# Rotary angles made on quarter rows during the gate products, and a reordered opening and attention fill, in a one-core hybrid-encoder kernel

## The chip, the core and the metric

The kernel runs on one core of a Trainium2 chip. The time is the device time of one execution, in microseconds (us); a figure for a kernel is the median of several executions. Engines are named as the profile names them: PE (TensorE, matrix products), PEld (its weight loads), DVE (VectorE), ACT (ScalarE), POOL (GpSimd) and SP (SyncE, which here only issues transfers). ACT and POOL issue transfers too. Each engine works through its instructions in order.

## The reference

One encoder layer over 512 tokens of width 2048, all in float32. h is the RMS-normalised input; one projection of h gives every branch its input. Branch A is a bidirectional state-space scan; branch B is attention with low-rank queries and keys and a rotary part; the two are gated, summed, projected and added to the input, with a last RMS norm.

```
h = rmsnorm(x, norm_w);  u = h @ w_in
z_ssm, xbc, dt_f, dt_b, q_a, kv_a, z_attn, g_ssm, g_attn = split(u)
y  = ssd(fwd) + flip(ssd(bwd)) + d_skip * xs
y  = grouped_rmsnorm(y * silu(z_ssm))
q  = rmsnorm(q_a) @ w_uq          # 16 heads x (128 plain + 64 rotary)
kv = rmsnorm(c_kv) @ w_ukv        # 16 heads x (128 key + 128 value)
qr, kr = apply_rope(qr, cos, sin), apply_rope(kr, cos, sin)   # ang = position * inv
o  = softmax((qn kn' + qr kr') / sqrt(192)) v * silu(z_attn)
out = rmsnorm(x + (sig(g_ssm)*(y @ w_ps) + sig(g_attn)*(o @ w_pa)) @ w_out)
```

## The kernel before, in words

Every float32 operand of a product is split into a rounded high part and the remainder (tile names ending in `_h` and `_l`, or `wh` and `wl`), and a product is three products of the parts. For a weight chunk (`wchunk`, L157 to L165; `w_split` later) SP loads `wraw` (512 KB, three buffers), ACT casts it to `wh` (L163 or L433), and DVE, or POOL in the very first chunks, subtracts to `wl` (L164 or L434). All activations are held transposed, 128 features by 512 tokens.

PE executes in the order in which the program is written. The other engines' instructions are put in order by a scheduler, by priority: program order, with some helpers moved ahead (`tc.high_priority`). `keep_in_program_order` pins one of them.

The stages, in the order of the program:

- **Opening** (L195 to L242). Four token tiles `xt` are loaded by SP in halves of 512 KB; ACT sums squares (L210) and takes the root (L185); DVE makes the reciprocal root with a Newton step (L187 to L191) and scales (L220), ACT scales the second half of the last two tiles (L218). PE transposes sixteen feature tiles into eight PSUM banks (`x_turn`, L225), and `x_out` evicts each on ACT (`h_h`, L229) and DVE (`h_l`, L230). Constants `cst` and `vec` are loaded ahead of x on ACT's queue. Then follows the product that gives the time steps, `dtp` (48 matmuls through L168 to L170).
- **xbc products and sums.** Six products `xbc`, their convolution, the sums of h that the next stage needs (`h_sums`), and `dt_make`, a chain of some 20 operations on 64 rows by 512 for the softplus of the time steps.
- **Gates.** Three 2048x2048 products by a Strassen scheme (`Strassen.pair`, products named P1, P5, P6, P2, P3, P7, P4, all through L579 to L581). In P5 each chunk of weights X is first changed in place by an accumulating transfer of POOL's queue, split by DVE, and then added to Y by DVE (L696), and in P6 to another chunk (L700).
- **State-space groups** 0 to 3, filled up on PE with xbc, qkv and za products (`fill`).
- **Rotary angles and attention's start** (L1140 to L1220). The positions are broadcast to 128 partitions, and DVE makes the angles, wraps them twice and ACT takes their sine and cosine (`sinT`, `cosT`, L1197 and L1199), with 120 units of fill between; k is rotated (`kra`, `krb`).
- **Attention**, 16 heads. For each of four token tiles `scores` (five matmuls into `s`, L1326 to L1330; maximum on DVE, exponential on ACT, sum and scaling `pr` on DVE, L1332 to L1337), then `trans` (four transposes of `pr` into `pb`, L1348, evicted by ACT and DVE), and `pv` with the head before. Between them `some(unit)` lets the fill queue issue so many matmuls: the coming heads' q and k products (`qk_gen`), the rotary q part (`rope_gen`) and the values (`v_gen`, 256 columns per matmul, L1265 to L1267). A head starts with `fill.until(("qk", hd))`. In the last two heads the queue is empty; then the first product of the next Strassen scheme is the fill. At head 14 the program loads and splits x11 and x12 of y (`xraw` tiles, cast on ACT into the tiles that the trace names x__12841 and x__13011).
- **Projections and output** by Strassen schemes again.

Of the kernel before, what the change touches and what calls it, by code (L numbers as in the profile page):

```python
# [18 lines left out]
P = 128  # L19
# [53 lines left out]
def build(tc, a):  # L73
# [46 lines left out]
    dt_d, kr_d = scratch("dt_d"), dr.tile([64, SEQ], F32, name="kr_d")  # L120

# [11 lines left out]
    act.dma_start(cst, a["cst"])  # L133
    act.dma_start(vec, a["vec"])
# [22 lines left out]
    def wchunk(src, n):  # L157
        with tc.high_priority(offset=ahead[0]):
            raw = wp.tile([P, 1024], F32, tag="wraw", bufs=3, name="wraw")[:, :n]
            nc.sync.dma_start(raw, src)  # L160
            h = wp.tile([P, 1024], F32R, tag="wh", bufs=3, name="wh")[:, :n]
            l = wp.tile([P, 1024], F32R, tag="wl", bufs=3, name="wl")[:, :n]
            act.copy(h, raw)  # L163
            (dve if ahead[0] else pool).tensor_sub(l, raw, h.bitcast(F32))  # L164
        return h, l  # L165
# [37 lines left out]
    for t in range(TT):  # L203
        xt = xp.tile([P, D], F32, name=f"xt{t}")
        ss = few(2)
        for i in range(2):
            cs = slice(i * D // 2, (i + 1) * D // 2)
            nc.sync.dma_start(xt[:, cs], a["x"][t * P:(t + 1) * P, cs])
            scr = xp.tile([P, D // 2], F32, tag="scr", bufs=1, name="scr")
            act.activation(scr, xt[:, cs], AF.Square, accum_out=ss[:, i:i + 1])  # L210
        v = few(1)
        dve.tensor_add(v, ss[:, 0:1], ss[:, 1:2])
        dve.tensor_scalar(v, v, 1.0 / D, EPS, ALU.mult, ALU.add)
        r = small_rsqrt(v, 1, lambda n: few(1))
        for i in range(2):
            cs = slice(i * D // 2, (i + 1) * D // 2)
            if t >= TT - 2 and i == 1:
                act.activation(xt[:, cs], xt[:, cs], AF.Copy, scale=r)  # L218
            else:
                dve.tensor_scalar_mul(xt[:, cs], xt[:, cs], r)  # L220
        xs_t.append(xt)
    tps = [mm(), mm(), mm(), pa(), pa(), pb(), pb(), pc()]

    def x_turn(k, t):
        pe.transpose(tps[k % 8][:, t * P:(t + 1) * P], xs_t[t][:, k * P:(k + 1) * P], ident)  # L225

    def x_out(k):
        nw = vec[:, V_NORM + k:V_NORM + k + 1]
        act.activation(h_h[:, k, :], tps[k % 8], AF.Copy, scale=nw)  # L229
        dve.scalar_tensor_tensor(h_l[:, k, :], tps[k % 8], nw, h_h[:, k, :].bitcast(F32), ALU.mult, ALU.subtract)  # L230

    for t in range(TT - 1):
        for k in range(8):
            x_turn(k, t)
    for k in range(8):
        x_turn(k, TT - 1)
        x_out(k)
    for k in range(8):
        tps[k] = (mm, mm, mm, pa, pa, pb, pb, pc)[k]()
        for t in range(TT):  # L240
            x_turn(8 + k, t)
        x_out(8 + k)  # L242
# [4 lines left out]

    def in_gemm(tile_i, n="mm"):
        return gemm(mm(n), win(tile_i), h_h, h_l)

# [19 lines left out]
    dtp = in_gemm(T_DT, "dtp")  # L270
    ahead[0] = AHEAD
    da_d = dr.tile([64, SEQ], F32, name="da_d")
    dv_, dt64 = sxd("dv_"), sxd("dt64")
    act.activation(dv_[0:64, :], dtp[0:64, :], AF.Identity, bias=vec[0:64, V_DTB:V_DTB + 1])
    act.copy(dv_[64:128, :], dtp[64:128, :])
    put(kr_d, dv_[64:128, :])

    def dt_make(new):

        v = dv_[0:64, :]  # L280
        e, u, pl, da64 = (new(n)[0:64, :] for n in ("e", "u", "pl", "da64"))
# [13 lines left out]
        dve.scalar_tensor_tensor(dt64[0:64, :], pl, 2.0, v, ALU.mult, ALU.add)  # L295
        dve.tensor_scalar_mul(an, an, -1.0)
        dve.tensor_scalar_mul(da64, dt64[0:64, :], an)
        act.copy(dt64[64:128, :], da64)
        act.dma_start(da_d[0:NH, :], da64[0:NH, :])
        chunked = lambda t: t[NH:64, :].rearrange("p (c l) -> p c l", c=TT)  # L300
        dve.tensor_mul(chunked(pl), chunked(dt64)[:, :, ::-1], an[NH:64, :].unsqueeze(2).broadcast_to([NH, TT, P]))
        act.dma_start(da_d[NH:64, :], pl[NH:64, :])
        put(dt_d, dt64)
# [97 lines left out]
    def za_gen(i):  # L401
# [3 lines left out]
        act.activation(g_, p_, AF.Silu)  # L405
# [422 lines left out]

    gates[2].hooks = {(1, "P3"): [dt_back], (1, "P7"): [h_back, lambda: [h_part("x21", 256, q) for q in range(2)]]}
# [42 lines left out]
    dve.tensor_scalar_mul(vneg, vec[:, V_SN + 8:V_SN + 16], -1.0)  # L872
# [940 lines left out]
```

## Time and profile before

| what | value |
|---|---|
| three runs | 2007.54, 2008.22, 2011.87 us; median 2008.22 |
| the profiled execution's own time | 2010.63 us |
| its span (first to last instruction) | 2008.8 us |
| mean granted PE clock | 0.992 |
| busy: PE, DVE, ACT, POOL | 1941.0, 1481.6, 1032.3, 250.1 us |
| moved by DMA | 382.78 MB, mean 191 GB/s |

The profiled execution spent 1.8 us outside its span, and it was 2.4 us slower than the median of the three runs. In rows of the timeline the first number is the start and the second the duration, both in us; what stands in brackets is how long the engine sat idle before, and whom it waited for. Matmuls are pipelined, so the time of one is the distance to the next start and not its duration.

### The profile page before, as it was taken

The page shows a single profiled execution, that of the slowest core. Times are in us where ns is not written, and L with a number is a line of the kernel's source. Part 1 is how long each engine was busy: PE and PEld are TensorE (multiplying, and loading weights), DVE is VectorE, ACT ScalarE, POOL GpSimd, SP SyncE. Part 2 cuts the span into 40 slices and gives each one's busy share as a digit, 9 for nine tenths or more (in the row PEclk, how much of TensorE's full clock was granted, in tenths as well). Part 3 has the DMA queues.
Part 4 walks back from the last instruction along what each step waited for, and adds up shares of the span by engine and source line. Part 5 has one row for each costly group of instructions (what it writes and reads, how often), then busy time and mean ns, then how long its engine had stood idle before and what let it go on. Part 6 is the DMA issues. An engine that isn't in the chain of part 4 may idle for free.

```text
span 2008.8 us, 24843 instructions
## 1 busy us (share of the span) xinstructions
PE 1941.0 (97%) x9026; PEld 1606.9 (80%) x9026; DVE 1481.6 (74%) x2064; ACT 1032.3 (51%) x1527; POOL 250.1 (12%) x315
## 2 busy tenths in 40 slices
PE   6999999999999999999999999999979999999997
PEld 4888888888878878887878788888867787888886
DVE  7976676676659879798794767666666898879466
ACT  6444445444464757757666344444444455444243
POOL 0001001001012020120200101112112111100011
PEclk9999999999999999999999999999989999999998
DMA  5468558558444635665454956877998687857446
GB/s 189 163 192 215 152 131 220 139 134 226 130 153 142 194 122 164 213 187 181 151 173 137 271 153 177 223 202 220 236 254 297 213 290 283 277 169 242 163 88 158
DMA packets 168907, 382.78 MB, mean 191 GB/s; under 512 B 16272, under 2 KB 65552, under 8 KB 168592
## 3 DMA queue, kind: packets, MB, share of 16 engines
q1 hardware_dynamic: 103248, 233.61, 35.3%
q0 software_dynamic: 30656, 103.30, 23.3%
q10 hardware_dynamic: 34880, 44.28, 6.2%
q8 instruction: 71, 1.16, 0.2%
q14 instruction: 52, 0.43, 0.1%
HBM read 329.22 MB, written 98.04 MB: 213 GB/s over the span
## 4 chain that ended last, share of the span: by engine, by line
PE 75%; DVE 10%; DMA 8%; issue 3%; ACT 3%; POOL 0%; SPq 0%; ACTq 0%; DVEq 0%; POOLq 0%
PE P L580 11%; PE P L581 11%; PE P L579 11%; PE xbc L168 3%; PE xbc L169 3%; PE xbc L170 3%; DMA wraw<-wps 2%; PE za L170 2%; PE za L168 2%; PE za L169 2%; PE qkv L168 1%; PE qkv L170 1%; PE qkv L169 1%; PE f L1582 1%; PE f L1581 1%
## 5 line engine op out<-in xcount | busy, mean ns | idle before, releaser
L433 ACT CAST wh<-X 128x1024 fp32r<-128x1024 f32 x164 | 172.9, 1056 | 198.4 <-PE P L581 152.2
L434 DVE TENSOR_TENSOR wl<-X,wh 128x1024 fp32r<-128x1024 f32 x164 | 200.1, 1224 | 91.2 <-ACT wh L433 90.8
L164 DVE TENSOR_TENSOR wl<-wraw,wh 128x1024 fp32r<-128x1024 f32 (+2 forms) x148 | 172.6, 1167 | 91.6 <-ACT wh L163 86.1
L163 ACT CAST wh<-wraw 128x1024 fp32r<-128x1024 f32 (+2 forms) x150 | 145.1, 970 | 120.3 <-PE xbc L169 37.7
L434 DVE TENSOR_TENSOR wl<-Y,wh 128x1024 fp32r<-128x1024 f32 x88 | 107.6, 1224 | 69.7 <-ACT wh L433 69.6
L168 PE MATMUL xbc<-h_h,wh 128*128 128x512 f32 x384 | 153.3, 399 | 0.0
L433 ACT CAST wh<-Y 128x1024 fp32r<-128x1024 f32 x88 | 92.8, 1056 | 115.9 <-PE P L581 105.8
L170 PE MATMUL xbc<-h_h,wl 128*128 128x512 f32 x384 | 150.3, 391 | 0.0
L169 PE MATMUL xbc<-h_l,wh 128*128 128x512 f32 x384 | 150.1, 391 | 0.0
L579 PE MATMUL P<-wh,h_h 128*128 128x512 f32 x384 | 149.4, 389 | 0.0
L580 PE MATMUL P<-wl,h_h 128*128 128x512 f32 x384 | 149.4, 389 | 0.0
L581 PE MATMUL P<-wh,h_l 128*128 128x512 f32 x384 | 149.4, 389 | 0.0
L433 ACT CAST wh<-wraw 128x1024 fp32r<-128x1024 f32 x68 | 71.8, 1055 | 120.4 <-PE P L581 63.5
L434 DVE TENSOR_TENSOR wl<-wraw,wh 128x1024 fp32r<-128x1024 f32 x68 | 83.2, 1224 | 66.5 <-ACT wh L433 66.5
L580 PE MATMUL P<-wl,S 128*128 128x512 f32 x288 | 112.3, 390 | 0.5 <-DVE wl L434 0.5
L579 PE MATMUL P<-wh,S 128*128 128x512 f32 x288 | 112.1, 389 | 0.0
L581 PE MATMUL P<-wh,S 128*128 128x512 f32 x288 | 112.1, 389 | 0.0
L170 PE MATMUL za<-h_h,wl 128*128 128x512 f32 x256 | 100.1, 391 | 2.0 <-DVE wl L164 2.0
L168 PE MATMUL za<-h_h,wh 128*128 128x512 f32 x256 | 101.6, 397 | 0.0
L169 PE MATMUL za<-h_l,wh 128*128 128x512 f32 x256 | 99.7, 389 | 0.0
L1335 ACT ACTIVATE pr<-s,nm 128x512 f32<-128x512 f32 x64 | 44.2, 690 | 82.9 <-DVE nm L1333 82.2
L170 PEld LDWEIGHTS xbc<-h_h,wl 128*128 128x128 f32 x384 | 72.3, 188 | 15.6
(748 smaller groups left out, 5188.6 us busy)
## 6 DMA issues: line engine op xcount, KB each, us to landing
wraw<-wi SPq DMA_DIRECT2D x102, 512.0 KB, 3.7
da<-da_d SPq DMA_DIRECT2D x64, 256.0 KB, 4.1
T_wps<-wps POOLq DMA_DIRECT2D x32, 512.0 KB, 9.5
T_wpa<-wpa POOLq DMA_DIRECT2D x32, 512.0 KB, 11.4
wraw<-wps SPq DMA_DIRECT2D x24, 512.0 KB, 6.7
wraw<-wo SPq DMA_DIRECT2D x20, 512.0 KB, 3.5
xbc_d<-xbc ACTq DMA_DIRECT2D x24, 256.0 KB, 2.3
wraw<-wun SPq DMA_DIRECT2D x16, 384.0 KB, 6.1
```

What stands on the lines that cost most here:

```text
L163: act.copy(h, raw)
L164: (dve if ahead[0] else pool).tensor_sub(l, raw, h.bitcast(F32))
L168: pe.matmul(out, wh, xh, start=start, stop=False)
L169: pe.matmul(out, wh, xl, start=False, stop=False)
L170: pe.matmul(out, wl, xh, start=False, stop=stop)
L433: i = act.copy(hi_, raw)
L434: dve.tensor_sub(lo_, raw, hi_.bitcast(F32))
L579: pe.matmul(bs[i], xh, wh, start=(j == 0), stop=False)
L580: pe.matmul(bs[i], xh, wl, start=False, stop=False)
L581: pe.matmul(bs[i], xl, wh, start=False, stop=(j == 7))
L1335: act.activation(pr, s, AF.Exp, bias=nm, scale=SCALE, accum_out=sm_)
L1581: pe.matmul(acc, mh, wl, start=False, stop=False)
```

## The change

It has five parts.

1. **Opening.** `cst` is loaded in two pieces and `vec` after x. The last tile of x comes in pieces of 1024, 512 and 512 columns. ACT takes the root directly from the last sum of squares, with the sums before it as bias. Seven PSUM banks take the transposes, and the eighth holds `dtp`, whose matmuls are written between the transposes of the later feature tiles. All remainders of chunks are made by DVE, none by POOL.
2. **dt_make** works on 128 rows by 256, after a transfer that moves half of the rows (`vd`).
3. **Angles.** They are made on 128 rows by 128 (four quarters of the tokens on four groups of 32 partitions), as a hook of the second gate, stored to DRAM in eight transfers of 32 rows, and loaded before attention by eight transfers of SP.
4. **Values.** `v_gen` issues matmuls of 512 columns, with the weights laid out anew.
5. **Fill.** The Silu of the za products has a higher priority. The rotary part and the values are queued later and in three pieces, a head waits for its q and k by running the fill at the expense of the units that follow, and the unit is 2.95, then 2.4, 1.7 and 2, and no longer 2.77 and 2.

```diff
-    act.dma_start(cst, a["cst"])
-    act.dma_start(vec, a["vec"])
+    act.dma_start(cst[:, :P], a["cst"][:, :P])
...
-            (dve if ahead[0] else pool).tensor_sub(l, raw, h.bitcast(F32))
+            dve.tensor_sub(l, raw, h.bitcast(F32))
...
+        edges = (0, 1024, 2048) if t < TT - 1 else (0, 1024, 1536, 2048)
...
+        act.activation(root, ss[:, i:i + 1], AF.Sqrt, bias=most, scale=1.0 / D)
+        dve.tensor_scalar(v, ss[:, i:i + 1], 1.0 / D, most, ALU.mult, ALU.add)
+        dve.reciprocal(r, root)
...
+    nc.sync.dma_start(vec, a["vec"])
...
+    BANKS = (mm, mm, mm, pa, pa, pb, pb)
...
+    dt_w.append(wchunk(a["wi"][T_DT, 0], 1024))
+    nc.sync.dma_start(cst[:, P:], a["cst"][:, P:])
+    for k in range(7):
         x_turn(k, TT - 1)
         x_out(k)
+    for k in range(7, KT):
         for t in range(TT):
+            x_turn(k, t)
+        x_out(k)
+        if k == 10:
+            dt_w.append(wchunk(a["wi"][T_DT, 1], 1024))
+        dt_mm(k - 7)
+    for k in range(KT - 7, KT):
+        dt_mm(k)
...
-    dtp = in_gemm(T_DT, "dtp")
+    act.dma_start(vd[64:128, 0:HS], dv_[0:64, 0:HS])
...
-        act.activation(g_, p_, AF.Silu)
+        with tc.high_priority(offset=ahead[0]):
+            act.activation(g_, p_, AF.Silu)
...
+        for qd in range(4):
+            act.dma_start(posi[qd * 32:(qd + 1) * 32].bitcast(I32),
+                          a["pos"][:, qd * P:(qd + 1) * P].broadcast_to([32, P]))
+        dve.tensor_copy(ang, posi.bitcast(I32))
...
+        for t, o, d in ((ang, sin_, sin_d), (ang2, cos_, cos_d)):
+            wrap(t)
+            act.activation(o, t, AF.Sin)
+            for qd in range(4):
+                act.dma_start(d[:, qd * P:(qd + 1) * P], o[qd * 32:(qd + 1) * 32])
+
+    gates[1].hooks = {(0, "P5"): [angles]}
...
-    act.activation(sinT, ang, AF.Sin)
-    wrap(ang2)
-    act.activation(cosT, ang2, AF.Sin)
-
-    fill.run(48)
+    for t_, d in ((sinT, sin_d), (cosT, cos_d)):
+        for qd in range(4):
+            nc.sync.dma_start(t_[qd * 32:(qd + 1) * 32, :], d)
...
+                pe.matmul(vp, ckv_h[:, k, tk], wh, start=(k == 0), stop=False)
+                pe.matmul(vp, ckv_h[:, k, tk], wl, start=False, stop=False)
+                pe.matmul(vp, ckv_l[:, k, tk], wh, start=False, stop=(k == 3))
...
-        if hd % 4 == 1 and hd < 12:
+        if hd % 4 == 2 and hd < 12:
             rv = chain(rope_gen(hd // 4 + 1), v_gen(hd // 4 + 1))
...
-        fill.until(("qk", hd))
-        unit = 2.77 if hd < AH - 2 else 2
+        while ("qk", hd) not in fill.done:
+            owed[0] -= fill.step()
+        unit = 2.95 if hd < AH - 5 else 2.4 if hd < AH - 3 else 1.7 if hd < AH - 2 else 2
```

How the order of the instructions moves is shown at three places.

The first is DVE in the opening, at the last tile of x: before, the small operations of the root (`small`), the scaling of half the tile (`xt`), and then at once the remainders `h_l` of the transposed tiles.

```order
L213 TENSOR_SCALAR small<-small 128x1
L187 RECIPROCAL small<-small 128x1
L188 TENSOR_TENSOR small<-small 128x1
L189 TENSOR_TENSOR small<-small 128x1
L190 TENSOR_SCALAR small<-small 128x1
L191 TENSOR_TENSOR small<-small 128x1
L220 TENSOR_SCALAR xt_288<-xt_288,small 128x1024
L230 SCALAR_TENSOR_TENSOR h_l<-mm,vec,h_h 128x512 x3
```

Now, at the same place:

```order
L217 TENSOR_SCALAR small<-small 128x1
L218 RECIPROCAL small<-small 128x1
L219 SCALAR_TENSOR_TENSOR small<-small 128x1
L220 TENSOR_SCALAR small<-small 128x1
L221 TENSOR_TENSOR small<-small 128x1
L222 TENSOR_SCALAR xt_286<-xt_286,small 128x1024
L164 TENSOR_TENSOR wl<-wraw,wh 128x1024
L241 SCALAR_TENSOR_TENSOR h_l<-mm,vec,h_h 128x512 x3
```

After the root there is one small operation less, and the remainder `wl` of the first dt chunk, which POOL made before, stands ahead of the first `h_l`.

The second is DVE in the first gate's P5 and P6, where `wl` is a chunk's remainder, and X an addition into the chunk that a later product reads. Before:

```order
L434 TENSOR_TENSOR wl<-X,wh 128x1024
L700 TENSOR_TENSOR X<-X,wraw 128x1024
L434 TENSOR_TENSOR wl<-X,wh 128x1024
L700 TENSOR_TENSOR X<-X,wraw 128x1024
L434 TENSOR_TENSOR wl<-X,wh 128x1024
L434 TENSOR_TENSOR wl<-wraw,wh 128x1024 x2
```

Now the angles' operations (`ta` and `tb`) stand between:

```order
L459 TENSOR_TENSOR wl<-X,wh 128x1024
L875 TENSOR_SCALAR ta<-ta 128x128
L725 TENSOR_TENSOR X<-X,wraw 128x1024
L876 TENSOR_TENSOR ta<-ta 128x128
L877 TENSOR_SCALAR ta<-ta 128x128
L878 TENSOR_TENSOR ta<-ta 128x128
L459 TENSOR_TENSOR wl<-X,wh 128x1024
L880 TENSOR_SCALAR ta<-ta 128x128
L725 TENSOR_TENSOR X<-X,wraw 128x1024
L459 TENSOR_TENSOR wl<-X,wh 128x1024
```

Although the program hooks the angles to the second gate, the scheduler has moved all 23 of their DVE operations up into the first gate, one to five between two remainders.

The third is head 14 of attention, where x11 and x12 are cast (`x__` tiles). On ACT before, with `pr` the exponentials of a token tile and `pt_h` the evicted transposes:

```order
L433 CAST x__12841<-xraw 128x1024
L1335 ACTIVATE pr,sm__12804<-s,nm 128x512
L433 CAST x__13011<-xraw 128x1024
L1335 ACTIVATE pr,sm__12826<-s,nm 128x512
L1350 CAST pt_h<-pb 128x4x128
L268 DMA o_x_216<-og 128x256
L268 DMA o_x_218<-og 128x256
L433 CAST x__13011<-xraw 128x1024
L433 CAST wh<-wraw 128x1024
L1350 CAST pt_h<-pb 128x4x128
L1335 ACTIVATE pr,sm__12878<-s,nm 128x512
```

Now:

```order
L1363 ACTIVATE pr,sm__12624<-s,nm 128x512
L1312 CAST kh<-kp 128x512
L458 CAST x__12673<-xraw 128x1024 x2
L458 CAST x__12843<-xraw 128x1024
L1378 CAST pt_h<-pb 128x4x128
L288 DMA o_x_218<-og 128x256
L288 DMA o_x_220<-og 128x256
L1378 CAST pt_h<-pb 128x4x128
L458 CAST x__12843<-xraw 128x1024
L1363 ACTIVATE pr,sm__12710<-s,nm 128x512
```

The exponentials of the first two token tiles now stand ahead of all four casts. That of the third tile still follows the last cast of x12, without a cast of weights between.

On PE in the same head before, there was no fill from its first scores to its third (`s`; `op` is the product with the values, its rows left out):

```order
L1329 MATMUL s<-kra,stack 128x512
L1330 MATMUL s<-krb,stack 128x512
L1348 MATMUL pb<-cst,pr 128x128 x4
L1326 MATMUL s<-kh,qh 128x512
L1327 MATMUL s<-kl,qh 128x512
```

Now:

```order
L1357 MATMUL s<-kra,stack 128x512
L1358 MATMUL s<-krb,stack 128x512
L168 MATMUL qp<-cq_h,wh 128x512
L169 MATMUL qp<-cq_l,wh 128x512
L170 MATMUL qp<-cq_h,wl 128x512
L1376 MATMUL pb<-cst,pr 128x128 x4
L168 MATMUL qp<-cq_h,wh 128x512
L169 MATMUL qp<-cq_l,wh 128x512
L170 MATMUL qp<-cq_h,wl 128x512
L1354 MATMUL s<-kh,qh 128x512
```

Three matmuls of head 15's q product now stand on each side of the transposes, and its whole k product, 12 matmuls, follows the second scores. Head 13 has 27 matmuls of fill from its first scores on, where it had 42.

More of the change, by code (lines that the diff above doesn't have):

```diff
@@ L120, in build @@
     dt_d, kr_d = scratch("dt_d"), dr.tile([64, SEQ], F32, name="kr_d")
+    sin_d, cos_d = (dr.tile([32, SEQ], F32, name=n) for n in ("sin_d", "cos_d"))
     m_d = {w: scratch(f"m_{w}", 2048) for w in ("x11", "x21")}
@@ L204, in build @@
         xt = xp.tile([P, D], F32, name=f"xt{t}")
-        ss = few(2)
-        for i in range(2):
-            cs = slice(i * D // 2, (i + 1) * D // 2)
+        edges = (0, 1024, 2048) if t < TT - 1 else (0, 1024, 1536, 2048)
+        ss = few(3)
+        for i, cs in enumerate(slice(*e) for e in zip(edges, edges[1:])):
             nc.sync.dma_start(xt[:, cs], a["x"][t * P:(t + 1) * P, cs])
-            scr = xp.tile([P, D // 2], F32, tag="scr", bufs=1, name="scr")
+            scr = xp.tile([P, D // 2], F32, tag="scr", bufs=1, name="scr")[:, :cs.stop - cs.start]
@@ L210, in build @@
             act.activation(scr, xt[:, cs], AF.Square, accum_out=ss[:, i:i + 1])
[L211 to L220, printed above, removed]
+            if i == 0:
+                most, v, root, r = (few(1) for _ in range(4))
+                dve.tensor_scalar(most, ss[:, 0:1], 1.0 / D, EPS, ALU.mult, ALU.add)
+            elif i < len(edges) - 2:
+                dve.tensor_scalar(most, ss[:, i:i + 1], 1.0 / D, most, ALU.mult, ALU.add)
@@ L232, in build, with dt_mm @@
+    dtp, dt_w = pc("dtp"), []
+    def dt_mm(k):
+        h, l = dt_w[k // 8]
+        cs = slice(k % 8 * P, (k % 8 + 1) * P)
+        mm3(dtp, h[:, cs], l[:, cs], h_h[:, k, :], h_l[:, k, :], k == 0, k == KT - 1)
     for t in range(TT - 1):
-        for k in range(8):
+        for k in range(7):
             x_turn(k, t)
-    for k in range(8):
+    dt_w.append(wchunk(a["wi"][T_DT, 0], 1024))
+    nc.sync.dma_start(cst[:, P:], a["cst"][:, P:])
+    for k in range(7):
         x_turn(k, TT - 1)
@@ L1305, in build @@
     rv = chain(rope_gen(0), v_gen(0))
-    for i in range(4):
+    for i in range(3):
         fill.add("rv", part(rv))
@@ L1310, in build @@
         fill.add(("qk", hd), qk_gen(hd))
-        if hd % 4 == 1 and hd < 12:
+        if hd % 4 == 2 and hd < 12:
             rv = chain(rope_gen(hd // 4 + 1), v_gen(hd // 4 + 1))
-        if hd < 12 and hd % 4:
-            for _ in range(2 if hd % 4 == 3 else 1):
-                fill.add(("rv", hd), part(rv))
+        if hd % 4 != 1 and hd <= 12:
+            fill.add(("rv", hd), part(rv))
     fill.until(("qk", 0))
```

133 lines of the change are left out of this document (66 added, 67 removed).

## The prediction

> **What bounds the kernel now.** I read the busy times first, then PE's waits summed by what ended them, and then the timeline, the windows and the transfers at the places of those waits.
>
> ```profile
> PE 1941.0 (97%) x9026; PEld 1606.9 (80%) x9026; DVE 1481.6 (74%) x2064; ACT 1032.3 (51%) x1527; POOL 250.1 (12%) x315
> ...
> PE mm L225 <- DVE xt L220: 19.8, 4, 11.6
> PE pb L1348 <- DVE pr L1337: 10.0, 2, 6.3
> PE P L580 <- DVE wl L434: 4.2, 9, 1.1
> PE vp L1265 <- ACT za L405: 2.7, 1, 2.7
> PE s L1326 <- ACT kh L1283: 2.5, 2, 1.2
> PE s L1327 <- DVE kl L1284: 1.9, 3, 0.7
> PE t L170 <- DVE wl L164: 1.3, 1, 1.3
> ```
>
> The first row is the page's, the others the waits of PE (us in total, times, longest). PE is the bound: of the span of 2008.8 us it is idle for 67.8. So a change pays in three ways only: it takes work from PE, it takes away one of these waits, or it spares the half-speed clock that follows a long one. DVE's 74% is an average: in some stages DVE is full, and there an added operation can become a wait of PE.
>
> **The opening.** Rows of the timeline (start, duration) of the last tile of x and what follows, the third being one line's group (shortest/median/longest):
>
> ```profile
> 9.55 0.20 ACT L185 ACTIVATE small<-small 128x1 f32<-128x1 f32 x1 [0.41 <-DVE small L213]
> 16.57 1.15 ACT L218 ACTIVATE xt<-xt,small 128x1024 f32<-128x1024 f32 x1
> ...
> L188 DVE TENSOR_TENSOR small<-small x2: 159/1131/2103, 15.8 to 20.0; 128x1 f32<-128x1 f32 x2
> ...
> 18.67 1.03 ACT L163 CAST wh<-wraw 128x1024 fp32r<-128x1024 f32 x1
> 19.60 0.20 ACT L185 ACTIVATE small<-small 128x1 f32<-128x1 f32 x1
> 19.78 4.64 POOL L164 TENSOR_TENSOR wl<-wraw,wh 128x1024 fp32r<-128x1024 f32 x2 [18.90 <-ACT wh L163]
> 22.17 2.27 DVE L189 TENSOR_TENSOR small<-small 128x1 f32<-128x1 f32 x1
> 24.86 0.75 DVE L220 TENSOR_SCALAR xt<-xt,small 128x1024 f32<-128x1024 f32 x1
> 26.90 2.07 DVE L230 SCALAR_TENSOR_TENSOR h_l<-mm,vec,h_h 128x512 fp32r<-128x512 f32 x3 [1.29 <-ACT h_h L229]
> 36.79 1.22 DVE L164 TENSOR_TENSOR wl<-wraw,wh 128x1024 fp32r<-128x1024 f32 x1
> ...
> 27.71 2.21 PE L225 MATMUL mm<-cst,xt 128*128 128x128 f32 x12
> 32.97 0.50 PE L168 MATMUL dtp<-h_h,wh 128*128 128x512 f32 x1
> 43.99 0.39 PE L168 MATMUL xbc<-h_h,wh 128*128 128x512 f32 x1
> ```
>
> POOL works from 19.78 to 24.42 on two remainders, and in that time two DVE operations on a single column took 2.10 and 2.27 us, where the same kind takes 0.16 elsewhere. So 2.10 + 2.27 - 0.32 = 4.05 us stand between the root at 19.60 and the scaling of the last tile at 24.86. With DVE making the remainders this goes. The root itself comes earlier by some 3.0: ACT no longer does the 1.15 of the third tile's scaling, three pauses of 0.41 ahead of a root go (the sum is now the root's bias), and I allow 0.6 for x landing sooner, now that most of the constants are loaded behind it (between 0 and 1). With 0.2 for one column operation less, the scaling starts at 24.86 - 7.25 = 17.6.
>
> Not all of that reaches PE. Before, the second set of transposes starts 2.85 after the scaling (27.71 - 24.86). Now the cast of the first weight chunk (1.03 on ACT) and its remainder (1.22 on DVE) stand ahead of the first evictions, and partly behind each other: I add 1.35 and take 4.2. Then PE has 36 transposes, each 0.164 (32 of them between 27.71 and 32.97), 5.9 us, and 48 dtp matmuls at 0.2296 (43.99 - 32.97, by 48), 11.0 us. So xbc starts at 17.6 + 4.2 + 16.9 = 38.7 and not at 43.99: **-5.3**. It is -3.5 if the weight chunk comes in the way with both of its steps and x lands no sooner, and -7.2 if the cast hides.
>
> **dt_make and the gates.** DVE from the opening to the gates, a window (busy time of each engine, clock, DMA share, GB/s), and rows of DVE:
>
> ```profile
> core 0: us, PE busy (x) PEld busy (x) DVE busy (x) ACT busy (x) POOL busy (x), PEclk, DMA share, GB/s
> 28.40:98.70 70.30, 70.29 (x320) 57.83 (x320) 68.98 (x79) 36.48 (x47) 0.00 (x0) 1.00 0.43 138
> ...
> 76.44 3.34 DVE L287 RECIPROCAL u<-u 64x512 f32<-64x512 f32 x1
> L292 DVE SCALAR_TENSOR_TENSOR pl<-pl,u 64x512 f32<-64x512 f32 x8 | 5.4, 678 | 0.1
> ...
> 121.69 1.22 DVE L434 TENSOR_TENSOR wl<-X,wh 128x1024 fp32r<-128x1024 f32 x1 [0.84 <-ACT wh L433]
> 125.09 1.23 DVE L434 TENSOR_TENSOR wl<-X,wh 128x1024 fp32r<-128x1024 f32 x1 [0.92 <-ACT wh L433]
> L1080 DVE SCALAR_TENSOR_TENSOR G<-cbb,dtT,G 128x128 f32<-128x128 f32 x128 | 40.1, 354 | 6.4 <-ACT G L1079 5.9
> ```
>
> DVE is full here (68.98 of 70.30 us). That counts, because PE comes to the gates 5.3 us sooner and DVE must, too. dt_make at half the width saves half of 3.34 and of 5.4, 4.4 us, and about 2.6 on the dozen shorter ones (my estimate from the same halving): 7 us, and DVE also starts its `h_l` some 6 us sooner. So DVE gains more than PE. The new transfer of half the rows (`vd`) makes the first operation wait; queued behind that one on DVE are the sums of h and the remainders of the xbc chunks, and PE waits for these. Where the scheduler has put that operation, two chunks of cover lie before (24 matmuls each, 11 us); I cost it at nothing, and its price without cover is in the third rival.
>
> The angles are 23 DVE operations on 128x128. Their price lies between 0.15 (an eighth of the 1.22 of 128x1024) and 0.354 (the row of L1080), 3.5 to 8.1 us in all; I take 0.25 a piece, nearer to the first because most have one input only. The scheduler puts them into the first gate, where DVE waits for ACT's `wh` by 0.84 and 0.92 a chunk. One or two between two remainders fit into that, five (1.25) don't, by 0.35. With three or four such places: **+1.0**, from 0 to +4 (8.1 less four or five pauses of 0.9). PE's own 4.2 us of waits for `wl` (L580) lie in this stage, so nothing else covers it.
>
> **Values, and the start of attention.** Rows of ACT, of PE, a window, and the transfers that feed `stack` (count, KB each, median us to land):
>
> ```profile
> 1152.13 0.63 ACT L1199 ACTIVATE cosT<-ang 128x512 f32<-128x512 f32 x1 [1.35 <-DVE ang L1192]
> 1159.05 0.60 ACT L405 ACTIVATE za<-za 128x512 f32<-128x512 f32 x1
> ...
> 1166.06 0.28 PE L1265 MATMUL vp<-wh,ckv_h 128*128 128x256 f32 x1
> 1169.89 0.28 PE L1267 MATMUL vp<-wh,ckv_l 128*128 128x256 f32 x1
> ...
> 1160.00:1165.00 5.00, 5.00 (x25) 5.00 (x25) 4.84 (x8) 2.55 (x4) 0.54 (x1) 0.50 0.94 288
> ...
> stack<-qr SPq DMA_DIRECT2D x64, 64.0 KB, 6.8
> ```
>
> A values matmul of 256 columns takes (1169.89 - 1166.06) / 32 = 0.1197, one of 512 columns 0.2296. 384 of the first become 192 of the second: 192 x (0.2394 - 0.2296) = **-2.0** us of PE's own work.
>
> ACT waited for the angles (1.35 ahead of `cosT`), `za`'s Silu came at 1159.05 behind that, and PE waited 2.7 us for the bank that it reads. After it the clock was 0.50 for 5 us: 25 matmuls that need 2.99 took 5.00, 2.0 lost. A wait of 1.3 for `wl` on the same full DVE stands before. With the angles out of this stage, and the Silu ahead in priority, 1.3 + 2.7 + 2.0 = **-6.0** go. What could stand in their place is the load of `sinT` and `cosT`: transfers of 64 KB take 6.8 us, and they are issued some 36 matmuls of fill (8.3 us) ahead. Bounds: -2 (only the clock) and -6.
>
> [...]
>
> In the heads between, PE waits for `kh` and `kl` 2.5 + 1.9 us, where a head's k product stands directly ahead of its scores. The new way of awaiting it, paid back from the units behind, draws the product forward in most heads but not in all: **-3.0**, from 0 to -4.4.
>
> **The last heads.** A window, and rows of PE and ACT:
>
> ```profile
> 1470.00:1510.00 40.00, 29.11 (x126) 23.32 (x125) 25.90 (x50) 18.30 (x32) 9.06 (x14) 0.87 0.90 239
> ...
> 1471.85 0.39 PE L1330 MATMUL s<-krb,stack 128*128 128x512 f32 x1
> 1480.25 1.09 PE L1348 MATMUL pb<-cst,pr 128*128 128x128 f32 x4 [3.68 <-DVE pr L1337]
> 1500.89 1.09 PE L1348 MATMUL pb<-cst,pr 128*128 128x128 f32 x4 [6.30 <-DVE pr L1337]
> ...
> 1493.83 1.05 ACT L433 CAST x__13011<-xraw 128x1024 fp32r<-128x1024 f32 x1 [5.43 <-DMA xraw<-yn_x]
> 1497.36 1.05 ACT L433 CAST wh<-wraw 128x1024 fp32r<-128x1024 f32 x1 [2.47 <-DMA wraw<-wps]
> ```
>
> PE is idle for 40 - 29.11 = 10.9 us, and at a mean clock of 0.87 another 29.11 x 0.13 = 3.8 are lost: 14.7. The exponential stood on ACT behind casts that waited for their loads, 5.43 and 2.47 us, with the DMA 0.90 busy. Now the exponentials of the first two tiles of head 14 stand ahead of the casts: the 3.68 goes, and its share of the lost clock (3.8 x 3.68 / 10.9 = 1.3). The third tile's still follows the last cast of x12. No cast of weights is between any longer (2.47 + 1.05 = 3.5), but PE comes there 3.7 us sooner, and the load not: that wait stays about as long. **-5.0**, from 0 to -14.7.
>
> **Sum.** -5.3 + 1.0 - 2.0 - 6.0 - 3.0 - 5.0 = -20.3 against the profiled execution: 2010.63 - 20.3 = 1990.3. It was 2.4 above the median of the three runs, so **1988** as a median.
>
> **The rivals.**
> - *The tail keeps all.* The loads are as late as before, PE meets the same stall of 14.7 at another tile. For it: the DMA's 0.90 and the unchanged chain of loads on SP; against it: the new order on ACT. The sum is -15.3: 1993. Chance 0.17.
> - *The tail's stall goes whole,* because the fill between the tiles (12 matmuls of the k product, 2.8 us, behind the second scores) covers the load's rest. -20.3 - 9.7 = -30.0: 1978. Chance 0.10.
> - *The opening is given back.* DVE is full up to 98.7, or the first operation of dt_make stands on DVE and waits for `vd`; then PE meets the same wall at the first gate. The sum is -15.0: 1993. Chance 0.10.
> - *The angles don't hide.* The change says second gate, the scheduler put them into the first; at 0.354 each with no pause used, 8.1 instead of 1.0 gives -13.2: 1995. Chance 0.04.
> - *Slower: the last two heads starve.* Head 13 has 27 matmuls of fill now and 42 before. From the end of a tile's scores (1471.85 + 0.39) to its transposes (1480.25) 8.0 us went by where ACT was blocked. The work in between is now, per tile, 5 matmuls of scores, 3 of the `op` product and some 7 of fill, 15 at 0.2296, and 1.09 of transposes: 4.5 us. If a late weight chunk blocks ACT at every tile of both heads, PE waits 8 x 3.5 = 28 us, and loses clock in the same proportion, 28 x 3.8 / 10.9 = 9.8: 37.8 in place of 14.7. With the other terms' -15.3 that is +7.8: 2016. It decides from 30 us of stall on (14.7 + 15.3), that is from 22 of waits or 6 blocked tiles of 8; before, two were. Chance 0.04.
>
> **How the numbers follow.** The forecast has the rest, 0.55: the middle of each term, 1988. All bounds together on the bad side (-3.5, +4, -2, -2, 0, 0) give -3.5 and 2005, on the good side (-7.2, 0, -2, -6, -4.4, -14.7) -34.3 and 1974. They don't fall together. The range from 1977 to 2000 takes in the forecast's own 1984 to 1994, the cases at 1978, 1993 and 1995 and a second miss beside these, and leaves out the slow rival. A difference of 0.2%, 4 us, is about the least that a measurement of this kernel tells from no change. Slower by more than that is the slow rival, and 0.01 for its half joined with bad bounds: 0.05. The same takes nearly all bad bounds together (2005), to which I give 0.04 out of the forecast and the near rivals. Faster is the rest, 0.91.
>
> **What would show it.** Right: `xbc` starts near 38.7 with no DVE column operation over 0.3 us in the opening; no `za` wait and no half clock between `cosT` and the first head; the wait for `pb` occurs once in head 14 and is about 6 us; waits for `P` at the gates grow by 1 at most. Wrong, step by step: `xbc` after 41; new waits of over 3 us for `wl` in the first gate; a wait for `sinT` or `cosT`; two or more long waits for `pb`. The prediction as a whole is wrong above 2000, and then the last heads would show more than 20 us of idle PE.

## The result, and the profile after

The changed kernel takes 1992.93 us (median of five runs, 1986.71 to 1993.25; before 2008.22, 2007.48 to 2011.87). The medians differ by 15.3 us; the ratio over all runs is 0.991, interval 0.9891 to 0.9929: 0.9% faster, 14 to 22 us. Forecast were 1988 and a range from 1977 to 2000. The total fits; of its terms one has the wrong sign.

The profiled execution took 1992.93 us too, its span 1991.1 (2008.8 before). PE's row of the page and PE's waits:

```profile
PE 1935.2 (97%) x8834; PEld 1596.1 (80%) x8834; DVE 1468.0 (74%) x2064; ACT 1029.8 (52%) x1527; POOL 246.2 (12%) x313
...
PE pb L1376 <- DVE pr L1365: 9.6, 1, 9.6
PE za L170 <- DVE wl L164: 6.0, 2, 5.0
```

All waits for `kh` and `kl` are gone, and that for the Silu of `za`. But `pb` still waits 9.6 us, now in one piece, and a wait of 5.0 for a weight remainder of `za` is new.

To see where the 17.7 us between the spans arise, I take the starts of the same matmuls in both traces. Before (the last product of the last state-space group, the first scores, the last `op`):

```profile
1043.81 0.88 PE L1091 MATMUL yb<-xT,G 128*128 128x64 f32 x6 [0.90 <-DVE y L1094]
1186.24 0.39 PE L1326 MATMUL s<-kh,qh 128*128 128x512 f32 x1
1529.16 0.39 PE L170 MATMUL op<-pt_h,v_l 128*128 128x512 f32 x1
```

And after, with the start of `xbc` (43.99 before) ahead of them:

```profile
39.33 0.39 PE L168 MATMUL xbc<-h_h,wh 128*128 128x512 f32 x1
...
1039.42 1.10 PE L1152 MATMUL yb<-xT,G 128*128 128x64 f32 x8 [1.66 <-DVE y L1155]
1183.61 0.39 PE L1354 MATMUL s<-kh,qh 128*128 128x512 f32 x1
1513.76 0.39 PE L170 MATMUL op<-pt_h,v_l 128*128 128x512 f32 x1
```

| stretch | measured, us | on record |
|---|---|---|
| opening, to `xbc` | -4.66 | -5.3 |
| from there to the last group (with the gates) | +0.27 | +1.0 |
| to the first scores (with a quarter of the values) | +1.76 | -6.0 - 0.5 |
| attention, to the last `op` (the rest of the values, heads, tail) | -12.77 | -1.5 - 3.0 - 5.0 |
| behind that | -2.3 | 0 |
| sum | -17.7 | -20.3 |

The third row is 8.3 us worse than forecast. The fourth and fifth are 5.6 better. Between these starts PE executes the same products in both traces, but for the halved number of `vp`. One trace of each kernel is compared here, and a stretch without any change differs between executions, too: behind the last `op` the fourteen traces of this document take 475.1 to 480.2 us, so the -2.3 is within that spread.

### The profile page after: what moved, and what is told of

It is laid out like the page before. It is cut to its first block, busy times and chain, and to the rows that moved or that the text cites. A ratio compares the mean times of both kernels' runs of the same rounds, so it can differ in the third digit from the quotient of the medians.

```text
span 1991.1 us, 24511 instructions
## 1 busy us (share of the span) xinstructions
PE 1935.2 (97%) x8834; PEld 1596.1 (80%) x8834; DVE 1468.0 (74%) x2064; ACT 1029.8 (52%) x1527; POOL 246.2 (12%) x313
## 4 chain that ended last, share of the span: by engine, by line
PE 76%; DVE 9%; DMA 7%; issue 5%; ACT 2%; POOL 1%; SPq 0%; ACTq 0%; DVEq 0%; POOLq 0%
PE P L605 11%; PE P L606 10%; PE P L604 10%; PE xbc L168 4%; PE xbc L169 4%; PE xbc L170 4%; PE za L170 2%; PE za L168 2%; PE za L169 2%; DMA wraw<-wps 2%; DVE sum L1131 2%; PE qkv L168 1%; PE qkv L170 1%; PE f L1609 1%; PE qkv L169 1%
```

## The experiments

Each experiment was timed in five rounds beside the kernel before on the same chip, where that kernel's medians were 2010 to 2011 us. So ratios to it are compared; 0.001 is 2 us.

**Where did the ahead-of-attention gain go?** In the changed kernel's trace, rows of ACT, POOL, DVE and PE:

```profile
1132.97 1.05 ACT L163 CAST wh<-wraw 128x1024 fp32r<-128x1024 f32 x1
...
1133.79 0.52 POOL L1401 DMA_DIRECT2D yn_S<-yn_S  x1 [19.08 <-DVE wl L164]
1134.33 0.54 POOL L1227 DMA_DIRECT2D k<-kr_d  x1
...
1137.83 0.50 POOL L1227 DMA_DIRECT2D k<-kr_d  x1
...
1142.50 0.69 DVE L1238 TENSOR_TENSOR o<-k,cosT 128x512 f32<-128x512 f32 x1 [7.75 <-DMA k<-kr_d]
1143.11 1.22 DVE L164 TENSOR_TENSOR wl<-wraw,wh 128x1024 fp32r<-128x1024 f32 x1
...
1144.38 0.80 PE L170 MATMUL za<-h_h,wl 128*128 128x512 f32 x1 [5.01 <-DVE wl L164]
...
1144.30:1150.10 5.80, 5.72 (x14) 4.52 (x15) 5.42 (x9) 3.82 (x7) 0.00 (x0) 0.50 0.99 214
```

The chunk's `wh` was ready at 1134.0. But the rotation of k (`o`) stands ahead of the remainder on DVE, and it waits 7.75 us for its operand, the first half of k (`k1`, loaded through L1227). POOL issues that in four parts from 1134.33 to 1137.83, behind a sum of y in DRAM (`yn_S`) of 1133.79. The sum lands at 1141.0, and the parts of k follow it one after the other, the first at 1141.2 and the one that `o` needs last at 1142.3. PE waits 5.01 us, and then 14 matmuls take 5.72 us at clock 0.50. Before, `k1` was no sooner (its last part below, landed at 1146.1):

```profile
1141.17 0.50 POOL L1166 DMA_DIRECT2D k<-kr_d  x1
...
1152.88 0.68 DVE L1204 TENSOR_TENSOR o<-k,cosT 128x512 f32<-128x512 f32 x1
```

There the angles' chain kept DVE busy until 1152.88, with remainders between, and k had landed by then. The work that was removed had been the cover of a late load.

*Angles alone.* The kernel before with only this part:

```diff
-    posi = aw.tile([P, SEQ], I32, tag="a", bufs=6, name="posi")
...
+    gates[1].hooks = {(0, "P5"): [angles]}
...
+            nc.sync.dma_start(t_[qd * 32:(qd + 1) * 32, :], d)
```

> The kernel before with the angles alone moved to the gates and loaded back. Theory A (without the angles' chain DVE reaches the rotation of k before k has landed, and everything queued behind it on DVE waits, a weight chunk's remainder among it): a new wait of PE of 3 to 6 us for such a remainder shortly before attention, with half clock behind it, in place of the waits there now; with some 0.6 more at the gates that is 2007 to 2012. Rival B (the record's reckoning: the stage loses its 6.0 us of stall): about 2008.2 - 6.0 + 1.0 = 2003, and no wait over 1 us there.

Measured: 2013.5, ratio 1.0014 (1.0003 to 1.0024), some 2.8 us slower. In its trace the same chain stands:

```profile
1147.57 0.69 DVE L1214 TENSOR_TENSOR o<-k,cosT 128x512 f32<-128x512 f32 x1 [6.59 <-DMA k<-kr_d]
1148.18 1.22 DVE L165 TENSOR_TENSOR wl<-wraw,wh 128x1024 fp32r<-128x1024 f32 x1
...
1149.45 0.80 PE L171 MATMUL za<-h_h,wl 128*128 128x512 f32 x1 [5.05 <-DVE wl L165]
```

Theory A holds: the new wait comes with the angles alone, whatever the fill. From the last state-space group to the first scores this trace takes 142.9 us, 0.5 more than the kernel before: the new wait has taken the place of the old ones. Taken by itself this part of the change loses time; where the rest of the 2.8 us is lost, the trace doesn't settle.

*k earlier.* The changed kernel with k loaded by SP, ahead of the compressed parts:

```diff
+    k1, k2 = (aw.tile([P, SEQ], F32, tag="kin", bufs=2, name=n) for n in ("k1", "k2"))
+    for qd in range(4):
+        nc.sync.dma_start(k1[qd * 32:(qd + 1) * 32, :], kr_d[0:32, :])
+        nc.sync.dma_start(k2[qd * 32:(qd + 1) * 32, :], kr_d[32:64, :])
     compressed(0, 6, rq_d, V_QN, cq_h, cq_l)
...
-        pool.dma_start(k1[qd * 32:(qd + 1) * 32, :], kr_d[0:32, :])
```

> The changed kernel with k's rotary rows loaded by SP into buffers of their own before the compressed parts, and no longer by POOL behind the sums in DRAM. Theory A (the 5.0 us wait of PE at 1144 is the rotation of k standing at the head of DVE's queue until k has landed): the wait goes, and the half clock behind it (2.7): 1992.9 - 7.7 = 1985. Rival B (the new loads of sine and cosine, or the weight chunk itself, are late in a full DMA): the wait stays over 3 us with cosT or the chunk as what it waits for, 1991 to 1993.

Measured: 1987.22, ratio 0.989 (0.987 to 0.991). PE's waits from 1100 to 1200 in its profiled execution, which was the longest of its six (1993.32, the shortest 1981.71):

```profile
PE t L168 <- ACT wh L163: 3.1, 1, 3.1
PE za L170 <- DVE wl L164: 0.8, 1, 0.8
```

The wait behind the rotation falls from 5.0 to 0.8: theory A's mechanism is shown. But the gain is only some 4 us against the changed kernel's 0.991, with overlapping intervals, because the next load, attention's first weight chunk, is late. In this trace and the next the wait for `pb` in the last heads is longer, too: 11.5 and 11.2 us in place of 9.6.

*Sine and cosine earlier, too.* In addition to the edit above their eight loads were moved ahead of the compressed parts:

```diff
+    for t_, d in ((sinT, sin_d), (cosT, cos_d)):
+        for qd in range(4):
+            nc.sync.dma_start(t_[qd * 32:(qd + 1) * 32, :], d)
     compressed(0, 6, rq_d, V_QN, cq_h, cq_l)
```

> The run before this one with sine and cosine, too, loaded by SP ahead of the compressed parts, so that SP comes to attention's first weight chunks sooner. Theory A (with k there in time, the rotary weights' chunk is late: SP issues it only at 1137 behind sine and cosine, and PE waits 3.1 us for it): the rest of the stall ahead of attention, 3.9 us of waits with 1 to 2 of clock, goes, ratio to the kernel before 0.986 to 0.987 where the run before had 0.989. Rival B (the DMA is full there with the sums in DRAM, and whoever comes late waits): the wait moves to another load of the stage, ratio 0.989.

Measured: 1988.5, 0.9897 (0.988 to 0.9914), and one wait:

```profile
PE za L168 <- ACT wh L163: 2.5, 1, 2.5
```

Rival B holds: the wait moves to the next load, a chunk of `za`. To see by what the DMA is filled, the sums of y were to be moved:

```diff
-    for step in sums(yn_d, slice(0, 2048)):
...
+        if hd == 1:
+            for step in sums(yn_d, slice(0, 2048)):
```

> The changed kernel with the sums of y in DRAM, which POOL issues ahead of the loads of k, moved to attention's head 1. Theory A (both stalls ahead of attention come from these sums: they hold POOL's queue in front of k and fill the DMA): k lands ahead of 1135, the wait of 5.0 us for a remainder behind the rotation goes, no other takes its place, 7 to 8 us less, 0.987. Rival B (the loads of the compressed parts and of the weights fill the DMA by themselves): a wait of 2 us or more for a weight chunk stays, 0.989 to 0.991.

Measured: 1994.27, 0.9912 (0.9889 to 0.9936). This edit tested nothing. On POOL the scheduler put the sums in the same places as before the edit, ahead of k, and the run is one more of the changed kernel, with the same wait of 4.95 us. It was done again with the instructions pinned, on top of two other edits, below.

**The last heads.** Rows of ACT, DVE, PE, SP and POOL in the changed kernel, a window behind the wait, and the transfers from 1455 to 1490 (median us to land at the end):

```profile
1479.82 1.04 ACT L458 CAST x__12843<-xraw 128x1024 fp32r<-128x1024 f32 x1 [6.14 <-DMA xraw<-yn_x]
...
1483.74 1.23 DVE L459 TENSOR_TENSOR wl<-wraw,wh 128x1024 fp32r<-128x1024 f32 x1 [1.54 <-ACT wh L458]
1484.88 0.48 DVE L1365 TENSOR_SCALAR pr<-pr,sm__12710 128x512 f32<-128x512 f32 x1
...
1485.51 1.09 PE L1376 MATMUL pb<-cst,pr 128*128 128x128 f32 x4 [9.56 <-DVE pr L1365]
...
1466.40 2.13 POOL L511 DMA_DIRECT2D T_wpa<-wpa  x2
1470.40 0.33 SPq L470 DMA_DIRECT2D xraw<-yn_x  x1
...
1485.50:1488.50 3.00, 2.99 (x10) 2.58 (x11) 2.50 (x5) 2.31 (x4) 0.00 (x0) 0.53 0.82 118
...
T_wpa<-wpa POOLq DMA_DIRECT2D x2, 512.0 KB, 13.0
```

The second half of x12 is issued at 1470.40 and is there at 1479.8, 9.4 us later, in a DMA that also carries two background additions of 512 KB (`T_wpa`, 13.0 us on the median) from 1466.4 on. ACT waits for it, ahead of the third tile's exponential. On DVE there is one more thing in the way: the remainder `wl` of the next weight chunk stands between the reciprocal of the tile's sum, ready at 1482.2, and the scaling of `pr` at 1484.88. DVE waits 1.54 us for that chunk's cast, and the remainder takes 1.2, so some 2.7 of the 9.6 us are this chunk's.

The half clock behind the wait lasts until 1488.3 and costs 3.00 x 0.47 = 1.4, so PE loses 11.0 in all. Before it was 10.9 of waits and, in two such stretches, 2.9 of clock: 13.8. The prediction's 14.7 took the mean clock over 40 us, in which the clock was 0.50 while PE stood idle, too (in the kernel before from 1497.0 to 1500.8, where PE executes nothing).

*No background additions at head 13.*

```diff
-            in_background(4 if hd < 8 else 6)
+            in_background(4 if hd < 7 else 6)
```

> The changed kernel with the last two of the 512 KB background additions in DRAM issued at head 7 and the following ones, and none at head 13. Theory A (the 9.6 us wait of PE at 1485 is ACT held up by the load of x12, which takes 9 us because those two additions fill the DMA): the load lands within 6 us, the wait falls to 4 to 6, with its clock 5 to 7 less, 0.988. Rival B (the sums of o and the weights fill the DMA anyway, or ACT is held up by the next weight chunk instead): the wait stays over 8 us, 0.991.

Measured: 1987.89, 0.9889 (0.9873 to 0.9905).

```profile
1464.12 0.33 SPq L470 DMA_DIRECT2D xraw<-yn_x  x1
...
1471.43 1.04 ACT L458 CAST x__12842<-xraw 128x1024 fp32r<-128x1024 f32 x1 [3.86 <-DMA xraw<-yn_x]
...
PE pb L1376 <- DVE pr L1365: 5.0, 1, 5.0
```

Theory A in direction: the wait falls from 9.6 to 5.0, and the ratio by 0.002, with overlapping intervals. But the load takes 7.3 us, not under 6, and that gives 2.1 of the 4.5 us. Another 1.2 come from its earlier issue, measured against PE, and 1.2 from the weight chunk, for which DVE waits 0.31 us here and not 1.54.

*Both edits,* early rotary loads and this one.

> Both edits together, early rotary loads and no background addition at head 13. If the two stalls are independent, the gains add: 0.9865 - 0.003 = about 0.983, 1976. If the time saved ahead of attention only brings PE sooner to the late load of x12, the wait there grows by what was saved: 0.987.

Measured: 1983.91, 0.9866 (0.9848 to 0.9885). Waits from 1100 to 1520:

```profile
PE pb L1376 <- DVE pr L1365: 5.6, 1, 5.6
PE za L168 <- ACT wh L163: 2.3, 1, 2.3
```

The time is that of the second expectation (0.987; the interval leaves out 0.983), but not for its reason: the wait for `pb` grows by 0.6 only. The first expectation had counted on 0.9865 for the early loads, which measured 0.9897. By the measured ratios the gains do add: 0.9897 + 0.9889 - 0.991 = 0.9876. The ratio is 9 us under the changed kernel's, and its interval ends below the point where the changed kernel's begins.

*The sums of y pinned,* one step in each of heads 1 to 6, on top of both:

```diff
+        if 1 <= hd <= 6:
+            for f in y_sums[hd - 1]:
+                tc.keep_in_program_order(f())
```

> The run with both edits, and the sums of y in DRAM pinned in program order on POOL, one step in each of attention's heads 1 to 6. Theory A (these sums fill the DMA ahead of attention, so that whatever is loaded there comes late): the DMA share from 1105 to 1140 falls under 0.8, the wait of 2.3 us for a weight chunk goes with its half clock, 4 us less, 0.9846. Rival B (the compressed parts, the weights and the rotary loads fill the DMA by themselves): share still about 1.0, the wait stays over 1.5 us, 0.986 to 0.987. Rival C (the sums now hold up POOL's background additions or fill the DMA in attention): the gain ahead of attention comes, and new waits for pr or kh in heads 1 to 14 take it back, 0.986 to 0.988.

Measured: 1983.15, 0.9865 (0.9847 to 0.9882). The stage ahead of attention in the changed kernel, then in this one:

```profile
1105.00:1140.00 35.00, 34.37 (x152) 28.10 (x150) 17.91 (x24) 11.74 (x17) 6.11 (x10) 1.00 0.99 294
```

```profile
1105.00:1140.00 35.00, 35.00 (x156) 29.00 (x155) 24.26 (x34) 15.51 (x23) 1.14 (x2) 1.00 0.68 226
...
PE op L169 <- DVE pt_l L1379: 1.8, 1, 1.8
```

The DMA share falls from 0.99 (1.01 with both edits, in the same window) to 0.68, and the stage has no wait left, so the sums do fill it: theory A's mechanism. From the last state-space group to the first scores this trace takes 134.5 us, where the kernel before took 142.4 and both edits 140.8. That is the size of gain that the prediction put on this stretch, but with the loads and the sums moved, too, and in one trace. Attention takes 3.4 us longer than with both edits, 2.1 of it in head 2 with the new wait of 1.8: rival C in part. The profiled execution is 4.4 us shorter than that of both edits, the median 0.8 and the ratio the same; so how much is given back stays open.

**Attention's heads.** *Fill alone* (values, Silu, new fill, on the kernel before):

```diff
+        with tc.high_priority(offset=ahead[0]):
...
+            yield 3
...
+        unit = 2.95 if hd < AH - 5 else 2.4 if hd < AH - 3 else 1.7 if hd < AH - 2 else 2
```

> The kernel before with the values of 512 columns, the Silu's priority and the new fill of attention. Theory A (the fill is worth what the two traces differ by): heads 1 to 12 lose 8 us less, values 2.4 less, the last heads 3 less, and the 2.7 us wait for the Silu with its half clock goes, 4.7: together 18, 1990. Rival B (the record's terms, 3.0 + 2.0 + 5.0, and the wait for the Silu stays, since DVE's angles hold ACT up there as before): 1998.

Measured: 1994.51, 0.9928 (0.9915 to 0.9942), 14.5 us faster, between the two. The wait for the Silu is still there with 1.3 us. Most of the change's gain comes from this part: 10.2 us of its trace's gain lie in attention.

*The unit as before.*

```diff
-        unit = 2.95 if hd < AH - 5 else 2.4 if hd < AH - 3 else 1.7 if hd < AH - 2 else 2
+        unit = 2.77 if hd < AH - 2 else 2
```

> The changed kernel with the unit of fill of before, 2.77 and 2. Theory A (heads 1 to 12 run without waits because values and rotary parts are queued later and in other pieces): waits ahead of scores in heads 1 to 12 stay under 2 us together; more fill is left for the last heads or less by 6 matmuls, total within 2 us of the changed kernel, 0.990 to 0.992. Rival B (the unit of 2.95 does it): waits for kh and kl of 0.6 to 1.2 us return in several heads, 5 us or more, 0.994.

Measured: 1994.62, 0.9922 (0.9901 to 0.9943). PE's busy time in heads 1 to 11 and its longest wait from 1200 on:

```profile
1195.00:1425.00 230.00, 229.83 (x1101) 189.61 (x1100) 163.57 (x330) 103.25 (x209) 42.59 (x71) 1.00 0.85 221
...
PE s L1354 <- ACT kh L1312: 3.7, 1, 3.7
```

PE doesn't wait there with the old unit either, so theory A holds for these heads. The unit decides where the fill runs out: with the old one head 13's k product stands directly ahead of its scores and PE waits 3.7 us, at 1441. Attention takes 335.3 us in its trace, where the six others with the new unit and an unchanged tail take 330.2 to 333.4. In the whole time this doesn't show: the intervals overlap.

**The opening.** *Opening and dt_make alone:*

```diff
-    act.dma_start(cst, a["cst"])
...
+    BANKS = (mm, mm, mm, pa, pa, pb, pb)
...
+        dt_mm(k - 7)
```

> The kernel before with the opening and dt_make of the change alone. Theory A (each part keeps its own gain, but for the angles): xbc starts at 39.3 us and not at 43.99, about 4 us are still there at the state-space groups, so 2008.2 - 4.3 = 2004. Rival B (DVE, full up to the gates, gives the gain back): xbc at 39.3, but new waits for the chunks' remainders of 3 us or more ahead of the gates, and about 2008.

Measured: 2004.25, 0.9975 (0.9962 to 0.9987), 5 us faster, and `xbc` at 38.9: theory A. The three parts together make -5.0 + 2.8 - 14.5 = -16.7, the whole change 0.009 x 2008, 18.

*Only the remainders moved from POOL to DVE,* in the kernel before:

```diff
-            (dve if ahead[0] else pool).tensor_sub(l, raw, h.bitcast(F32))
+            dve.tensor_sub(l, raw, h.bitcast(F32))
```

> The kernel before with the two remainders of the dt chunks made by DVE and no longer by POOL, nothing else. Theory A (the two column operations of 2.1 and 2.3 us were slow only because POOL streamed beside them): they take 0.16 us, the last tile's scaling starts at 20.8 in place of 24.86, the remainders cost DVE 1.2 to 2.4 on the way, and xbc starts at 41 to 42.5 and not at 43.99; about 2 us faster, 0.999. Rival B (DVE was held by something else): the scaling stays at 24 to 25 and the time is the same or up to 2 us longer by the added work of DVE.

Measured: 2009.79, 0.9993 (0.9976 to 1.0009), not to be told from no change. Its rows:

```profile
21.08 0.16 DVE L188 TENSOR_TENSOR small<-small 128x1 f32<-128x1 f32 x1
21.28 0.16 DVE L189 TENSOR_TENSOR small<-small 128x1 f32<-128x1 f32 x1
22.88 0.75 DVE L220 TENSOR_SCALAR xt<-xt,small 128x1024 f32<-128x1024 f32 x1
...
42.01 0.39 PE L168 MATMUL xbc<-h_h,wh 128*128 128x512 f32 x1
```

The two column operations are back at 0.16, theory A; two remainders now stand between root and scaling, which so comes at 22.88 and not at 20.8, and `xbc` starts 2.0 sooner.

*POOL again, in the changed kernel* (the same line reversed):

> The changed kernel with POOL making the first remainders again, as before. Theory A (what POOL streams slows DVE's operations at the same time): DVE's h_l beside POOL's 2.3 us take 1.5 us or more instead of 0.69, or column operations 2 us, xbc starts at 41 to 42 and not at 39.3, and about 2 us are lost in all. Rival B (only the place of the two remainders on DVE's path counts): h_l keeps 0.7 us, the second set of transposes starts sooner, by up to 1.2, and xbc at 38 to 39.

Measured: 1990.67, 0.9907 (0.9891 to 0.9924).

```profile
19.82 2.35 POOL L164 TENSOR_TENSOR wl<-wraw,wh 128x1024 fp32r<-128x1024 f32 x1 [18.93 <-ACT wh L163]
20.35 2.07 DVE L241 SCALAR_TENSOR_TENSOR h_l<-mm,vec,h_h 128x512 fp32r<-128x512 f32 x3 [1.95 <-ACT h_h L240]
```

Rival B: `h_l` keeps 0.69 beside POOL's work, and `xbc` starts at 38.8; the time can't be told from the changed kernel's. What matters is that POOL's remainder no longer falls on the root's small operations.

## Why the prediction was right, and where it was wrong

- **Opening (-5.3, measured -4.66).** Right, with the terms as put. The scaling of the last tile starts at 17.55 (17.6 on record) and the second set of transposes 4.06 behind it (4.2). The stretch up to `xbc` then took 17.7 us and not 16.9. Two things in it were not foreseen, and they nearly cancel: up to 27 us the matmuls ran at half speed (0.43 apart, last two rows, for 0.23 elsewhere), so that the 48 took 13.4 us and not 11.0, and the 36 transposes took 4.3 and not 5.9. The lower bound of -3.5 is a slip: from the terms shown it is -3.8.

```profile
17.55 0.75 DVE L222 TENSOR_SCALAR xt<-xt,small 128x1024 f32<-128x1024 f32 x1
...
21.61 1.12 PE L236 MATMUL mm<-cst,xt 128*128 128x128 f32 x4 [1.50 <-DVE h_l L241]
22.95 0.63 PE L169 MATMUL dtp<-h_l,wh 128*128 128x512 f32 x1
23.38 0.63 PE L170 MATMUL dtp<-h_h,wl 128*128 128x512 f32 x1
```

- **Gates (+1.0).** The size fits (PE's waits from 44 to 570 us grow from 0.5 to 1.4), the cause was not right. The 4.2 us of waits for `wl` that the prediction placed in this stage are the whole program's; 0.5 of them lie here. The stretch's +0.27 confirms nothing: with small changes or none it takes 998 to 1003 us in the traces. The angles' operations cost 0.22 to 0.29 each, as taken, but what PE waited for there is the load of the positions, at the head of DVE's queue:

```profile
114.99 0.23 DVE L862 CAST ta<-tb 128x128 f32<-128x128 int32 x1 [4.73 <-DMA tb<-pos]
...
117.25 0.50 PE L605 MATMUL P<-wl,S 128*128 128x512 f32 x1 [1.37 <-DVE wl L459]
```

- **Start of attention (-6.0, measured with its share of the values +1.76).** This is the step that failed: "With the angles out of this stage, and the Silu ahead in priority, 1.3 + 2.7 + 2.0 = -6.0 go." Those waits went, and a wait of 5.01 with half clock behind it came. (The old half clock was read too short: it lasted from 1159.0 to 1165.8 and cost about 3, not 2.) The prediction asked what else could stand in their place and looked only at the new loads, `sinT` and `cosT`; k's old load, with the sums ahead of it on POOL, was in the trace of before at 1141. Its bounds, -2 and -6, left out a loss for which there was a row. Of the +1.76 itself some 1.7 is no part of that: behind a wait of 1.66 at the last group (1039.42) the clock was 0.5 for 3.4 us, which this place doesn't have in the trace of before. Such stretches come and go: with the code of before this stretch takes 142.4, 137.6 and 141.6 us in three traces (before, opening alone, remainders on DVE), with that of the change 142.2 to 145.2 in five. So it is sure that the 6.5 did not come, but how much slower the stage became is not.
- **Values (-2.0).** 192 matmuls fewer stand in PE's row of the page, as put. In attention, with three quarters of them, the distances from their starts to the next sum up to 35.2 us before and 33.8 now: -1.4, for the -1.5 on record.
- **Heads (-3.0; with the tail and the values -12.77).** Too small, and for the wrong reason. Of the -12.77, 1.4 are the values' and 2.8 the tail's (below), which leaves some 8.5 to the heads. In the window from 1200 to 1440 PE was idle for 5.75 us before and for none after; the matmuls around a wait stood further apart as well, which adds 1.7; about 1 us has no row:

```profile
1200.00:1440.00 240.00, 234.25 (x1247) 197.46 (x1246) 162.42 (x327) 104.51 (x211) 40.67 (x67) 1.00 0.81 215
```

```profile
1200.00:1440.00 240.00, 240.00 (x1148) 198.33 (x1147) 169.29 (x339) 107.90 (x215) 45.56 (x74) 1.00 0.83 220
```

  The prediction gave the credit to the new way of awaiting a head's q and k. In the trace of the changed kernel at most 9 matmuls stand between the last transposes of a head and the next head's first scores, the usual unit, so that loop had nothing to issue; before, there are 18 of 512 columns at head 8 and 24 at head 12, so `until` had to drain 9 and 15 there. The run with the old unit excludes the unit as the cause in these heads. What is left is the queue's new order (rotary and values later, in three pieces). That is by exclusion; no run has it alone.
- **Tail (-5.0, measured 11.0 - 13.8 = -2.8).** The new order did what was put: the wait of the first tiles is gone, and one is left. But that one is 9.6 us and not about 6. The prediction had saved 3.5 by the cast of weights that no longer stands on ACT; the remainder of the same kind of chunk still stands on DVE, ahead of `pr`, and holds it by some 2.7. So the truth lies between the forecast and the first rival (the stall stays whole at another tile). That rival's time, 1993, is that of the median, but by luck: through the other terms' errors, which cancel.
- **The slow rival** did not come: one tile of the last eight waits, not six.

So the total was right by luck: a miss of 8.3 stood against 5.6 of gains that were larger than taken, and 2.3 of these lie behind attention, where the program is the same and the traces differ by as much.

## What to carry to other kernels

Before work is taken off an in-order engine, look at what stands next in its queue and when that one's inputs land: the removed work may have been the cover of a load, and then everything queued behind is late, as a remainder was here behind a rotation that waited 7.75 us on DVE. Time saved ahead of attention, where the DMA was full (0.99 from 1105 to 1140 in the changed kernel), went in part to the next late load: the wait of 5.0 behind k became one of 3.1 for a weight chunk, and then one of 2.5 for another. Moving traffic that is not urgent out of such a stage took its waits away (with the sums in DRAM pinned in attention the share was 0.68 and no wait was left), but whether it pays in the whole depends on where it goes: here the total didn't change measurably. And read the built order after such an edit, since a scheduler may put the instructions back where they were.

The best version here is the changed kernel with the early rotary loads and without background additions at head 13: 0.9866 (0.9848 to 0.9885) of the kernel before, about 1984.

## What the runs showed of the hardware

- The length of a wait alone didn't decide on the half clock. At the same place of two kernels, the changed one and the one with the sums pinned, a wait of 1.66 us was followed by a mean clock of 0.72 in the next 6 us, and one of 2.25 by 1.00:

```profile
1039.40:1045.40 6.00, 5.98 (x24) 5.02 (x25) 4.47 (x15) 5.22 (x9) 0.00 (x0) 0.72 0.39 131
```

```profile
1036.80:1042.80 6.00, 5.93 (x31) 5.11 (x32) 4.49 (x16) 5.17 (x9) 0.00 (x0) 1.00 0.40 134
```

  The first stretch has 24 matmuls, the second 31. What else counts was not shown.
- In the clock records of two traces the stretches of half clock between 40 and 1900 us last 3.4, 6.8, 3.4, 6.8 and 3.4 us (before, from 582.1, 1159.0, 1479.8, 1496.9 and 1558.3) and 3.4, 3.4, 6.8 and 10.2 us (changed, from 576.9, 1041.2, 1143.6 and 1478.1). At 0.50 one of 3.4 costs a busy PE 1.7. By my estimate such stretches are a large part of why executions of one kernel differ, by 11.6 us with k earlier: there the two longest (1993.32, 1993.03) had mean clocks of 0.993 and 0.992, the two shortest (1981.71, 1983.37) 0.995 and 0.996, and 0.003 of 1990 is 6 us. No run tested it by itself.
- Work of POOL did not slow every operation of DVE beside it. Beside a remainder of 2.3 us on POOL two operations on one column, which read SBUF alone, took 2.1 and 2.3 us in the kernel before, and 0.16 each with those remainders on DVE; three of 128x512 that read PSUM, too, took 0.69 each in the changed kernel with POOL's remainders.
